# One encoder layer in float32 on one core: the stores to HBM move from the load queue to ScalarE's queue

## The chip, the cores and the metric

The kernel runs on one core of a Trainium2 chip. The metric is device time in microseconds (us) of one execution; the time of the kernel before is the median of three runs. A core has five engines, each with its own in-order instruction stream: TensorE (PE, matmuls), VectorE (DVE), ScalarE (ACT), GpSimd (POOL) and SyncE (SP), which computes nothing and here issues the DMA transfers. An instruction that waits for a semaphore holds up everything behind it in its own stream, and nothing in the others.

## What is computed

One layer, applied to a prompt of 1024 tokens and a sample of 512 tokens with the same weights, everything in float32. The core of the reference:

```
h = rms_norm(x, pre_g);  z = h @ w_in                       # 2048 -> 5632
q, k, v, g_attn, u, vg, g_gmlp = split(z)
q, k = rope(q), rope(k)                                     # 8 heads of 128, 2 kv heads
a = window_attention(q, k, v, sink) * silu(g_attn)          # band of 3 blocks of 128, a sink logit
m = spatial_gating(gelu(u), gelu(vg), ln, ws, bs) * silu(g_gmlp)
y = concat([a, m]) @ w_out                                  # 2048 -> 2048
x = x + rms_norm(y, post_g)
x = x + sigmoid(x @ w_pg) * (p @ w_pe)
```

## The kernel before

All arrays lie transposed, features on the 128 partitions and the 1536 tokens of both sequences along the free dimension, in two halves of 768 tokens. The large products go through five sweeps, "a", "b" and "c" (parts of w_in), "y" (w_out) and "p" (w_pg). Each sweep takes its product as a two by two block product with seven block products (the tables `A_OF` and `B_OF` say which quarters are added or subtracted for each, `ORDER` in which order they run). An item is one output pair in one of the seven products: TensorE runs 8 k-tiles by 2 token groups by 3 matmuls into one PSUM tile `ps...` (two of them exist). The three matmuls (lines 171 to 173) are the float32 product from a high and a low part of each operand: ScalarE copies a tile into a rounded high part (line 163), VectorE subtracts to get the low part (line 165, seen as L155).

Around each item stand, on other engines:

- the weights of the item three ahead (`make_weights`): two loads into `wr...` (4 buffers), GpSimd adds or subtracts them, then the split into `wt...` (3 buffers);
- the operands of the next product (`fetch_operand`, `split_operand`): two loads into `ar...`, VectorE adds, then the split into `a...` (8 buffers) as each k-tile is done with;
- the product's way out of PSUM (`leave_product`): ScalarE copies to `u...` or `v...` (lines 255, 269, 275) and VectorE adds, which gives outputs `o...`; from there, by kind, rope (VectorE and GpSimd), Gelu, Silu, squares, transposes, and then a store to a scratch tensor in HBM (`q`, `k`, `v`, `gu`, `vg`, `y`) or to the output.

Attention and the spatial gating run as small jobs between the items of sweeps "b" and "c". They load what earlier sweeps stored (`aq`, `ak`, `av`, `vn`, `gm`) and store their own results (`at<-ao`, `gum<-mx`). In sweep "p" the tiles `x2` (residual plus normed y) are made and stored as well (`x<-x`). At the start the kernel makes p @ w_pe into scratch tensors (`pe<-pe`), and the normed x (`h<-x`, `h<-xb`).

The order of everything is fixed when the kernel is built: the class `Line` keeps a clock of TensorE's planned time and runs the jobs that are due; each job is a generator that yields the time it expects its step to take. So the place of an instruction in its engine's stream is the planner's estimate of when its inputs are ready.

All DMA goes out from SyncE: `load` at line 139 issues on `nc.sync`, and `store` is the same function (line 142). Both kinds therefore stand in one stream, in the planner's order: 1374 loads and 304 stores. The framework adds the waits: a store waits for the engine that made its data; a load waits until its buffer is free; and each DMA takes one of eight completion counters in turn (`DMAHW0` to `DMAHW7` in the listings below) and waits until the DMA that had that counter before it, eight places back, has landed.

Of the kernel before, what the change touches and what calls it, by code (L numbers as in the profile page):

```python
# [96 lines left out]
def tile_encoder_layer(ctx: ExitStack, tc: tile.TileContext, xT, pT, wall, pre_g, post_g, sink,  # L97
                       ln_g, ln_b, wsT, bs, cos, sin, mask, out):
    nc = tc.nc
# [39 lines left out]
    def load(dst, src):  # L139
        nc.sync.dma_start(out=dst, in_=src)  # L140

    store = load

    ident = const.tile([P, P], F32, tag="ident", name="ident")
    make_identity(nc, ident)
# [821 lines left out]
```

## Time and profile before

| | |
|---|---|
| three runs | 2611.05 us median (2610.92 to 2614.11) |
| the profiled execution | 2611.79 us, of which its span from the first to the last instruction 2610.0 us |
| TensorE busy | 2503.3 us, 96% of the span |
| VectorE, ScalarE, GpSimd busy | 1703.8 us (65%), 958.4 us (37%), 736.8 us (28%) |
| DMA | 643.63 MB through one queue, packets take 72.7% of the 16 engines' span, 247 GB/s from and to HBM |

Busy time counts the engine's own work. Waiting and the issuing of DMAs by a sequencer are not in it, so SyncE has no busy time at all; its waits are a view of their own. Idle time of an engine other than TensorE costs something only where TensorE then waits for it.

### The profile page before, as it was taken

What the parts mean: (1) busy time and instruction counts of PE and PEld (TensorE: products, weight loads), DVE (VectorE), ACT (ScalarE), POOL (GpSimd) and SP (SyncE); (2) the same over time, 40 slices, a digit from 0 to 9 for tenths busy, and PEclk for the clock granted to TensorE, in tenths of its full rate; (3) what the DMA queues carried; (4) which work ended last, traced back from release to release, by engine and by line L of the source; (5) the groups of instructions that cost most, each with busy time, mean ns of one, the idle gap of its engine ahead of it and who ended that gap; (6) DMA issues with size and microseconds to landing.
All of it is one profiled execution on the core that took longest, in us unless ns stands there. A gap on an engine that the chain in (4) does not pass through costs nothing.

```text
span 2610.0 us, 36511 instructions
## 1 busy us (share of the span) xinstructions
PE 2503.3 (96%) x14268; PEld 2462.0 (94%) x14268; DVE 1703.8 (65%) x1883; ACT 958.4 (37%) x1378; POOL 736.8 (28%) x316
## 2 busy tenths in 40 slices
PE   5998999999999999999999999999999999999998
PEld 5998999999989999999999999999999999999998
DVE  3657566766667757777767665465566876666773
ACT  3142222323675543333546732332232223322321
POOL 4164324355012202302222013112310321433434
PEclk8999999999999999999999999999999999999999
DMA  6967776666575679879656677566577987879885
GB/s 228 360 237 239 259 248 218 202 206 235 181 263 183 186 245 298 308 252 308 211 173 223 215 269 256 211 224 222 171 233 253 332 302 287 284 246 318 306 301 204
DMA packets 372109, 645.97 MB, mean 248 GB/s; under 512 B 29280, under 2 KB 211680, under 8 KB 371936
## 3 DMA queue, kind: packets, MB, share of 16 engines
q1 hardware_dynamic: 371936, 643.63, 72.7%
q8 instruction: 112, 1.84, 0.3%
q14 instruction: 61, 0.50, 0.1%
HBM read 533.43 MB, written 110.10 MB: 247 GB/s over the span
## 4 chain that ended last, share of the span: by engine, by line
PE 71%; DVE 12%; ACT 5%; issue 5%; POOL 3%; DMA 3%; SPq 0%; POOLq 0%; DVEq 0%; ACTq 0%
PE psy L172 5%; PE psy L173 5%; PE psy L171 5%; PE psp L172 5%; PE psc L173 5%; PE psc L172 5%; PE psp L173 5%; PE psc L171 5%; PE psp L171 5%; PE psa L172 4%; PE psa L171 4%; PE psa L173 4%; PE psb L172 3%; PE psb L173 3%; PE psb L171 3%
## 5 line engine op out<-in xcount | busy, mean ns | idle before, releaser
L171 PE MATMUL psa<-aa,wta 128*128 128x384 f32 x896 | 304.8, 340 | 9.0 <-DVE oa L152 5.2
L172 PE MATMUL psa<-aa,wta 128*128 128x384 f32 x896 | 304.2, 339 | 3.2 <-DVE aa L155 3.2
L171 PE MATMUL psy<-ay,wty 128*128 128x384 f32 x896 | 303.1, 338 | 4.1 <-ACT ay L163 4.1
L171 PE MATMUL psc<-ac,wtc 128*128 128x384 f32 x896 | 305.9, 341 | 1.0 <-ACT ac L163 1.0
L172 PE MATMUL psp<-ap,wtp 128*128 128x384 f32 x896 | 301.6, 337 | 4.6 <-DVE ap L155 4.6
L172 PE MATMUL psy<-ay,wty 128*128 128x384 f32 x896 | 303.1, 338 | 2.2 <-DVE ay L155 2.2
L171 PE MATMUL psp<-ap,wtp 128*128 128x384 f32 x896 | 301.5, 337 | 3.8 <-ACT ap L163 3.8
L172 PE MATMUL psc<-ac,wtc 128*128 128x384 f32 x896 | 301.5, 337 | 1.7 <-DVE ac L155 1.7
L173 PE MATMUL psa<-aa,wta 128*128 128x384 f32 x896 | 303.0, 338 | 0.0
L173 PE MATMUL psy<-ay,wty 128*128 128x384 f32 x896 | 302.3, 337 | 0.0
L173 PE MATMUL psc<-ac,wtc 128*128 128x384 f32 x896 | 301.4, 336 | 0.0
L173 PE MATMUL psp<-ap,wtp 128*128 128x384 f32 x896 | 300.8, 336 | 0.0
L171 PE MATMUL psb<-ab,wtb 128*128 128x384 f32 x672 | 230.7, 343 | 0.5 <-DVE ua L152 0.5
L172 PE MATMUL psb<-ab,wtb 128*128 128x384 f32 x672 | 226.2, 337 | 2.5 <-DVE ab L155 2.5
L173 PE MATMUL psb<-ab,wtb 128*128 128x384 f32 x672 | 225.9, 336 | 0.0
L171 PEld LDWEIGHTS psa<-aa,wta 128*128 128x128 f32 x896 | 170.9, 191 | 10.7 <-issue 4.8
L172 PEld LDWEIGHTS psa<-aa,wta 128*128 128x128 f32 x896 | 170.9, 191 | 5.6 <-DVE aa L155 5.4
L172 PEld LDWEIGHTS psp<-ap,wtp 128*128 128x128 f32 x896 | 169.3, 189 | 6.7 <-DVE ap L155 6.4
L171 PEld LDWEIGHTS psy<-ay,wty 128*128 128x128 f32 x896 | 170.6, 190 | 4.9 <-ACT ay L163 4.8
L172 PEld LDWEIGHTS psy<-ay,wty 128*128 128x128 f32 x896 | 170.5, 190 | 4.1 <-DVE ay L155 3.8
L171 PEld LDWEIGHTS psp<-ap,wtp 128*128 128x128 f32 x896 | 169.3, 189 | 4.9 <-ACT ap L163 4.7
L172 PEld LDWEIGHTS psc<-ac,wtc 128*128 128x128 f32 x896 | 169.5, 189 | 2.5 <-DVE ac L155 1.9
(254 smaller groups left out, 5432.3 us busy)
## 6 DMA issues: line engine op xcount, KB each, us to landing
wrc<-wall SPq DMA_DIRECT2D x96, 512.0 KB, 7.0
arb<-h SPq DMA_DIRECT2D x96, 384.0 KB, 6.1
arc<-h SPq DMA_DIRECT2D x96, 384.0 KB, 5.5
wry<-wall SPq DMA_DIRECT2D x72, 512.0 KB, 6.0
wrp<-wall SPq DMA_DIRECT2D x72, 512.0 KB, 7.2
arp<-x SPq DMA_DIRECT2D x88, 384.0 KB, 5.8
wra<-wall SPq DMA_DIRECT2D x60, 512.0 KB, 5.7
ara<-h SPq DMA_DIRECT2D x80, 384.0 KB, 5.4
```

What stands on the lines that cost most here:

```text
L171: nc.tensor.matmul(ps, lhsT=l[0], rhs=r[0], start=start, stop=False)
L172: nc.tensor.matmul(ps, lhsT=l[0], rhs=r[1], start=False, stop=False)
L173: nc.tensor.matmul(ps, lhsT=l[1], rhs=r[0], start=False, stop=stop)
```

## The change

The name `store` becomes a function of its own, which issues on ScalarE's queue. Loads stay on SyncE.

```
@@ -139,7 +139,8 @@
     def load(dst, src):
         nc.sync.dma_start(out=dst, in_=src)
 
-    store = load
+    def store(dst, src):
+        nc.scalar.dma_start(out=dst, in_=src)
```

The streams of TensorE, VectorE and GpSimd keep their instructions and their order. SyncE loses 304 DMAs (1678 become 1374), and ScalarE's stream grows from 1284 to 1588 rows. The eight completion counters are still dealt out over all DMAs in program order, loads and stores together. Line numbers after line 142 are one higher in the changed kernel.

On SyncE near the end of the p @ w_pe stage, before the change (names with `h` or `pe` on the left are stores to scratch tensors, `wra_1` are the weights of the second item of sweep "a"):

```order
L140 DMA pe_1_132<-pe_1_869 128x768 [waits DMAHW5_49,DVE_49]
L140 DMA h_4_168<-x_12_354 128x768 [waits DMAHW6_49]
L140 DMA pe_0_133<-pe_0_887 128x768 [waits DMAHW7_49,DVE_49]
L140 DMA wra_1_10_903<-wall 128x4x128 [waits DMAHW0_49,Activation_49]
L140 DMA wra_1_10_903<-wall 128x4x128 [waits DMAHW1_49]
L140 DMA wra_1_11_906<-wall 128x4x128 [waits DMAHW2_49,Activation_49]
L140 DMA wra_1_11_906<-wall 128x4x128 [waits DMAHW3_49]
L140 DMA h_5_169<-x_13_356 128x768 [waits DMAHW4_49]
```

The same place on SyncE after the change:

```order
L140 DMA sin<-sin 128x1024 [waits DMAHW3_49]
L140 DMA wra_1_10_903<-wall 128x4x128 [waits DMAHW5_49,DVE_49]
L140 DMA wra_1_10_903<-wall 128x4x128 [waits DMAHW6_49]
L140 DMA wra_1_11_906<-wall 128x4x128 [waits DMAHW4_49,DMAHW0_49,Pool_49]
L140 DMA wra_1_11_906<-wall 128x4x128 [waits DMAHW2_49]
L140 DMA wra_2_10_1039<-wall 128x1024 [waits DMAHW2_49,DMAHW0_49,Pool_49]
```

The stores between the table `sin` and the weights are gone from this stream; the loads still wait for completion counters, which stores on the other queue hold in between.

On ScalarE in the second product of sweep "a" (number 5 in `ORDER`; `va` are copies out of PSUM, `wta` splits of weights), before:

```order
L269 ACTIVATE va_1952<-psa_3_1871 128x768
L163 ACTIVATE wta_6_1978<-wra_6_11_1892 128x1024
L269 ACTIVATE va_2030<-psa_4_1948 128x768
L163 ACTIVATE wta_7_2060<-wra_7_11_1968 128x1024
L269 ACTIVATE va_2108<-psa_5_2026 128x768
```

The same stretch after (`q` is a rope result from GpSimd, `h` a normed x tile from VectorE):

```order
L270 ACTIVATE va_1952<-psa_3_1871 128x768 [waits PE_49]
L143 DMA q_0_188<-oa_5_1878 128x768 [waits DMAHW4_49,Pool_49]
L143 DMA h_6_186<-xb_1867 128x768 [waits DMAHW7_49,DVE_49]
L164 ACTIVATE wta_6_1978<-wra_6_11_1892 128x1024
L143 DMA h_7_187<-xb_1912 128x768 [waits DMAHW6_49,DVE_49]
L270 ACTIVATE va_2030<-psa_4_1948 128x768 [waits PE_49]
L143 DMA q_0_188<-oa_5_1954 128x768 [waits DMAHW7_49,Pool_49]
L143 DMA h_0_180<-xb_1944 128x768 [waits DMAHW0_49,DVE_49]
L164 ACTIVATE wta_7_2060<-wra_7_11_1968 128x1024 [waits DMAHW2_49]
L143 DMA h_1_181<-xb_1990 128x768 [waits DMAHW5_49,DVE_49]
L270 ACTIVATE va_2108<-psa_5_2026 128x768 [waits DMAHW3_49,PE_49]
```

Two stores now stand ahead of each copy out of PSUM or each split, and each waits for VectorE or GpSimd.

On ScalarE at the end of the fifth product of sweep "a" (number 4 in `ORDER`; `aa` are splits of the next product's operands, `oa_4_3854` a Gelu whose result TensorE transposes), before:

```order
L275 ACTIVATE va_2183<-psa_6_3781 128x768
L163 ACTIVATE aa_0_3868<-ara_0_10_3361 128x768
L529 ACTIVATE oa_4_3854<-oa_4_3854 128x768
L163 ACTIVATE wta_1_3880<-wra_1_00_3804 128x1024
L163 ACTIVATE aa_1_3883<-ara_1_10_3428 128x768
```

The same place after:

```order
L276 ACTIVATE va_2183<-psa_6_3781 128x768 [waits DVE_49]
L143 DMA q_0_190<-oa_4_3785 128x768 [waits DMAHW4_49,Pool_49]
L164 ACTIVATE aa_0_3868<-ara_0_10_3361 128x768 [waits PE_49]
L530 ACTIVATE oa_4_3854<-oa_4_3854 128x768 [waits DMAHW6_49]
L164 ACTIVATE wta_1_3880<-wra_1_00_3804 128x1024 [waits DMAHW7_49,DMAHW6_49,Activation_49]
L164 ACTIVATE aa_1_3883<-ara_1_10_3428 128x768 [waits PE_49]
```

One store of a rope result, which waits for GpSimd, has come in ahead of the burst of operand splits.

## Rows read from the trace of the kernel before

**Rows 1.** The page, busy time of each engine, share of the span, instructions.
```profile
PE 2503.3 (96%) x14268; PEld 2462.0 (94%) x14268; DVE 1703.8 (65%) x1883; ACT 958.4 (37%) x1378; POOL 736.8 (28%) x316
```

**Rows 2.** Waits of TensorE: who waited for whom, us in total, times, longest.
```profile
PE pspe L171 <- ACT pa L163: 11.7, 1, 11.7
PE ss_x L291 <- POOL accx L152: 11.6, 2, 10.4
PE s L172 <- DVE ks L155: 8.6, 8, 2.1
PE t L652 <- ACT p L645: 5.4, 19, 1.6
...
PE psa L171 <- DVE oa L152: 5.2, 2, 4.5
```

**Rows 3.** Waits of SyncE's own queue, same columns.
```profile
SPq L140 <- ACT ao L676: 200.8, 22, 15.9
SPq L140 <- DVE x L152: 115.6, 32, 9.5
...
SPq L140 <- POOL op L152: 78.4, 16, 10.4
```

**Rows 4.** Line 140: DMA instructions, duration ns min/median/max, first and last start us.
```profile
L140 SPq DMA_DIRECT2D pe<-pe x32: 319/504/1896, 18.8 to 115.6; - x32
...
L140 SPq DMA_DIRECT2D gum<-mx x32: 319/320/596, 992.4 to 1225.2; - x32
```

**Rows 5.** Timeline from 95 us: start, length, engine, instruction, [idle before <- releaser].
```profile
95.54 3.39 SPq L140 DMA_DIRECT2D wra<-wall  x4
...
103.94 2.40 POOL L155 TENSOR_TENSOR wra<-wra,wra 128x1024 f32<-128x1024 f32 x1 [29.94 <-DMA wra<-wall]
...
106.38 1.06 ACT L163 ACTIVATE wta<-wra 128x1024 fp32r<-128x1024 f32 x1 [31.27 <-POOL wra L155]
...
107.47 1.23 DVE L155 TENSOR_TENSOR wta<-wra,wta 128x1024 fp32r<-128x1024 f32 x1 [3.31 <-ACT wta L163]
...
108.61 1.81 DVE L385 COPY pe<-pspe 128x768 f32<-128x768 f32 x2
...
109.71 0.41 PE L171 MATMUL psa<-aa,wta 128*128 128x384 f32 x1 [2.38 <-ACT aa L163]
```

**Rows 6.** Windows: stretch, engines' busy us (instructions), clock, DMA share, GB/s.
```profile
80.00:107.00 27.00, 27.00 (x158) 26.87 (x156) 18.12 (x21) 0.62 (x1) 2.40 (x1) 1.00 0.99 372
```

**Rows 7.** Timeline, 238 to 248 us.
```profile
238.68 0.81 ACT L269 ACTIVATE va<-psa 128x768 f32<-128x768 f32 x1 [6.56 <-PE psa L173]
...
243.10 2.59 DVE L428 SCALAR_TENSOR_TENSOR xb<-xb,pre_sb,rb_x 128x768 f32<-128x768 f32 x1
...
245.73 0.96 DVE L155 TENSOR_TENSOR ara<-ara,xb 128x768 f32<-128x768 f32 x1
...
246.61 0.95 DVE L152 TENSOR_TENSOR oa<-ua,psa 128x768 f32<-128x768 f32 x1
```

**Rows 8.** Timeline from 464 us.
```profile
464.31 0.84 ACT L163 ACTIVATE aa<-ara 128x768 fp32r<-128x768 f32 x1
464.49 2.44 POOL L152 TENSOR_TENSOR oa<-oa,rbq 128x768 f32<-128x768 f32 x1
465.04 0.84 ACT L529 ACTIVATE oa<-oa 128x768 f32<-128x768 f32 x1
...
466.42 0.81 PE L492 MATMUL tnvg<-ident,oa 128*128 128x128 f32 x6
...
466.96 0.32 SPq L140 DMA_DIRECT2D q<-oa  x1
```

**Rows 9.** Timeline in attention, 763 to 774 us.
```profile
763.12 0.32 SPq L140 DMA_DIRECT2D gu<-ob  x1
...
767.45 0.63 ACT L577 ACTIVATE qs<-aq 128x512 fp32r<-128x512 f32 x1 [0.87 <-DMA aq<-q]
...
773.25 0.45 PE L172 MATMUL s<-ks,qs 128*128 128x384 f32 x1 [2.09 <-DVE ks L155]
```

## The prediction

> **What bounds the kernel now.** I read the page first. TensorE is busy 2503.3 of 2610.0 us [rows 1], so all that any change of queues can win is its idle time, some 107 us, and whatever is lost must show up there too. The next view is TensorE's waits [rows 2]: the two longest, 11.7 us for the first split of the kernel and 11.6 us for GpSimd's sum of squares, hang on the start of the kernel and on a chain of adds, and no store stands in them. Of the rest, 8.6 us is attention's scores waiting for VectorE's low part of k, 5.4 us transposes waiting for ScalarE's scaled probabilities, 5.2 us a product waiting until VectorE has read PSUM. No row has TensorE waiting for a DMA directly, so a load counts only through the engine that works on it.
>
> Then SyncE's own waits [rows 3]. Here the reader is to see how long the single stream stands before a store: 200.8 us in 22 cases for the attention output, 115.6 us in 32 for the x2 tiles, 78.4 us in 16 for outputs finished on GpSimd, the longest single stand 15.9 us. Everything behind, loads included, waits that long. The change takes these stands out of SyncE's stream and puts them into ScalarE's, which is busy only 37% [rows 1], but on which every operand split, every weight split and half of the copies out of PSUM stand in order.
>
> **What goes and what it is worth.** SyncE's loads may now pass a store that isn't ready. Not freely: each DMA still waits for the one eight places back, and where that is a store, the load waits for its landing. So a load gains up to seven places. Whether that reaches TensorE I looked up where TensorE stood and a late load was behind it.
>
> The end of the first stage is one [rows 5]. SyncE issues the four loads of the second item's weights at 95.54 us, GpSimd, which has stood 29.94 us for them, adds at 103.94, ScalarE splits at 106.38, VectorE takes the low part at 107.47 and only then, behind it in order, the two copies out of PSUM at 108.61, for which TensorE waits 2.38 us. With the loads earlier the split is no longer held by GpSimd; it is then held by the stores that now stand ahead of it on ScalarE. In that stretch the 16 DMA engines are busy 99% of the time at 372 GB/s [rows 6], so a store of 384 KB is moved in about 1 us and the loads can't simply come in between. Bounds: 0, when the same bytes lie ahead, and 2.38, when the wait goes altogether; I take the middle, 1.2.
>
> The Trainium skill, page "DMA: Bandwidth & Descriptors", section "Issuing engines are not separate DMA queues", speaks against this gain: DMAs started on several engines run on the same 16 DMA engines and interleave, and the only thing saved is the time to start them. By that rule this term and the next are 0 and the sum below is 2.2 us higher. The trace has both cases: the 99% stretch agrees with it, and the 15.9 us stand is not one of transfer at all.
>
> The other is in attention [rows 9]. A store of a Gelu result leaves SyncE at 763.12, the loads of q and k right behind it; ScalarE waits 0.87 us for them, and the scores wait 2.09 us on TensorE. Bounds 0 and 2.09, near the row where the DMA is named as the releaser (0.87): taken 1.0. In the other blocks the splits of q and k come long after their loads, so I count nothing more of the 8.6 us.
>
> **What is added to ScalarE.** 304 DMA instructions. On SyncE such a store holds the sequencer 0.32 us in the median when the queue is free and 0.50 us when it is crowded [rows 4]; no DMA was issued from ScalarE before, so this is the nearest row, and 0.33 us is what I take. The total, 304 by 0.32 to 0.50, is 97 to 153 us in a stream with some 1650 us of idle time, and weight splits run up to two items ahead of their use, so nearly all of it is hidden. What isn't hidden are the waits, and only where the next instruction on ScalarE is one that TensorE needs at once. I laid the new order of ScalarE over the times of its old instructions and of the stores' producers. Three places come out.
>
> First, the second product of sweep "a" [rows 7]. VectorE is behind there and runs without a gap. A store of normed x ahead of the copy `va` needs VectorE's x tile, which ends at 245.69 us; the copy, 238.68 before, can then start only at 245.69 + 0.33 + some wake-up = 246.1 and ends at 246.9. VectorE wants its result at 246.61. So of the 7.4 us by which the copy slips VectorE's lateness takes up 7.1, and 0.3 us come out. The same pattern one item earlier gives another 0.3 to 0.4. TensorE waits for just this VectorE instruction (the 5.2 us row of rows 2 has it). Together +0.7; bounds 0 and 5 times 0.5 = 2.5, with each of the five items hit at the dearer issue price.
>
> Second, the burst of splits at the end of the fifth product [rows 8]. The store of a rope result comes in ahead of the split at 464.31. GpSimd finishes that tile at 464.49 + 2.44 = 466.93; with 0.33 for the issue the split starts at about 467.3, 3.0 us late, and so does all behind it. The Gelu at 465.04 then ends at 468.9 in place of 465.9, and TensorE, which began its six transposes at 466.42, would begin them 2.5 us later. VectorE's low parts move along, so nothing catches up before the next product. +2.5; bounds 0 (if the loads that are no longer held let GpSimd finish sooner) and 3.0.
>
> Third, attention. In each of the 24 blocks a store of the output stands among short steps that follow each other closely: the transposes wait 5.4 us in 19 cases already [rows 2], a mean of 0.3 us, so there is no room there. Where the store falls between the Exp of the sink and the scaled probabilities, 0.33 us goes through to TensorE; I find that in about one block in four, 6 by 0.33 = +2.0; bounds 0 and 24 by 0.5 = 12.
>
> In the last sweep weight splits slip by some microseconds, since stores of outputs wait for GpSimd in front of them (78.4 us over 16 cases on SyncE [rows 3]). An item is 48 matmuls, and 2503.3 us by 14268 [rows 1] is 0.175 us each, so 8.4 us; a split that may run from two items ahead has up to 16.8 us of cover, and I count nothing. If that cover were gone, the 78.4 us would come down on TensorE. The last store of the kernel moves to an idle ScalarE: 0.
>
> **The sum.** −1.2 − 1.0 + 0.7 + 2.5 + 2.0 = +3.0 us on the profiled execution's own 2611.79 us (2610.0 of span and 1.8 around it) gives 2614.8. That execution is 0.74 us above the median of the runs shown, so against the median the forecast is 2614.0 us, 0.1% more. About 0.2%, 5.2 us, is what a measurement of this kernel can tell from no change: 2605.8 to 2616.3 counts as the same.
>
> **Rivals.** A, faster: the loads were the hidden cause of more than I grant. Breaking the stands lets GpSimd and VectorE run ahead everywhere, and the waits that hang on them shrink: the 2.38 us, the 5.2 us, the 8.6 us. Together 16.2; with 5.2 of costs still paid, 2611.05 − 16.2 + 5.2 = 2600. For it: stands of 200.8 us in attention alone. Against: in nearly all blocks ScalarE's splits are not waiting for a load.
>
> B, slower: the convoy. Where VectorE has no idle time, ScalarE waits for VectorE at a store, and VectorE then waits for the copy or split behind that store, so that each store of the early rope and x tiles opens a gap in the engine that was the bound there. Some 36 such stores (16 of x, 20 of q and k) at 0.5 us are 18 us: 2629. It decides from the point where VectorE's lateness no longer covers ScalarE's slip; at 246.61 it covers 7.1 of 7.4 us. For it: the margin is that thin. Against: behind 270 us VectorE has idle time again.
>
> C, it doesn't do what it says: since a load still waits for the DMA eight places back, and its buffer often was a store's source, SyncE is held by the same stores as before, only a little later, and ScalarE's waits lie in its idle time: 2611.
>
> **How the numbers follow.** Forecast 0.43, with its own range 2608 to 2619; A 0.20; B 0.25; C 0.12. Faster by over 0.2%: A alone, 0.20. Slower: B and about a quarter of the forecast's range (2616.3 to 2619), 0.25 + 0.11 = 0.36. Same: the rest, 0.44. For 8 in 10 the range has to reach to near the middle of A and past B's price, since 12 us stood as the upper bound of attention alone: 2602 to 2632.
>
> **What would show it.** In the changed kernel's profile a second hardware queue has the 304 stores, and SyncE's list of waits no longer has `ao`, `op` or the x2 tiles. TensorE's wait at 109.7 us is about 1.2 us or less, the one near 773 us under 1.1. Near 466 us the transposes wait some 2.5 us where they began without a wait. GpSimd's waits for weights fall. The waits on `t` go up by about 2 us. I am wrong if TensorE's waits move by more than 6 us in total in either direction; if DMA instructions on ScalarE take 0.6 us or more; or if TensorE waits for weight splits anywhere in the last sweep.

## The result, and the profile after

The changed kernel takes 2627.71 us in the median of six runs (2619.0 to 2630.7); the kernel before took 2610.99 us in six runs beside them. The ratio is 1.0056 (the two medians alone would give 1.0064), with a 95% interval of 1.0038 to 1.0073: the change makes the kernel slower by about half a per cent. The forecast was 2614.0 us, so the direction on which it was built is right and the size is not: 16.7 us came instead of 3.0. The profiled execution took 2629.63 us.

The page after, engines as in [rows 1], then the two hardware queues (packets, MB, share of the 16 engines' span):

```profile
PE 2504.5 (95%) x14268; PEld 2462.5 (94%) x14268; DVE 1694.8 (64%) x1883; ACT 958.8 (36%) x1378; POOL 751.6 (29%) x316
...
q1 hardware_dynamic: 306144, 533.51, 61.3%
q10 hardware_dynamic: 65792, 110.12, 11.2%
```

TensorE works as long as before (2504.5 us for 2503.3). Its idle time is the span less that: 2627.8 − 2504.5 = 123.3 us, where it was 2610.0 − 2503.3 = 106.7. The 16.6 us between them are nearly all of the 17.8 us by which the span grew, so the question is which waits grew. The waits of TensorE after, to be laid beside [rows 2]:

```profile
PE pspe L172 <- DVE pe L386: 16.3, 8, 12.8
...
PE t L653 <- ACT p L646: 10.7, 17, 3.5
...
PE psp L173 <- DVE ap L156: 7.6, 8, 4.0
PE s L173 <- DVE ks L156: 7.0, 7, 2.6
PE psa L173 <- DVE aa L156: 6.4, 9, 2.0
PE psa L172 <- DVE oa L153: 6.0, 2, 4.6
PE tnvg L493 <- ACT oa L530: 4.4, 2, 2.4
```

The first row is new in its size: a single wait of 12.84 us at the start, in the p @ w_pe stage, where it was 3.04 before:

```profile
31.04 0.44 PE L171 MATMUL pspe<-pa,wtpe 128*128 128x384 f32 x1 [3.04 <-DVE pe L385]
```

SyncE's stream did lose the stands of [rows 3]; in their place stand others, some on the landing of the very stores that left:

```profile
SPq L140 <- DVE wta L156: 95.6, 29, 8.4
SPq L140 <- DMA gum<-mx: 81.5, 19, 11.1
SPq L140 <- POOL wra L153: 79.4, 19, 12.1
```

And a store on ScalarE costs what [rows 4] let expect, 0.33 us (line 143, duration ns min/median/max):

```profile
L143 ACTq DMA_DIRECT2D pe<-pe x32: 326/326/389, 30.3 to 120.4; - x32
...
L143 ACTq DMA_DIRECT2D at<-ao x24: 366/377/417, 667.1 to 1521.4; - x24
```

**The start.** The timeline from 14 us after, ScalarE's own rows and those of SyncE, VectorE and TensorE that matter:

```profile
14.74 2.29 ACT L321 ACTIVATE sq<-x 128x768 f32<-128x768 f32 x3
...
17.27 0.96 DVE L386 COPY pe<-pspe 128x768 f32<-128x768 f32 x1 [1.37 <-PE pspe L174]
...
20.98 4.72 SPq L140 DMA_DIRECT2D wra<-wall  x4
...
30.31 0.35 ACTq L143 DMA_DIRECT2D pe<-pe  x1
30.71 0.84 ACT L321 ACTIVATE sq<-x 128x768 f32<-128x768 f32 x1 [13.67 <-DMA wra<-wall]
...
38.06 1.04 ACT L164 ACTIVATE wtpe<-wrpe 128x1024 fp32r<-128x1024 f32 x1
...
41.28 0.69 PE L172 MATMUL pspe<-pa,wtpe 128*128 128x384 f32 x1 [12.84 <-DVE pe L386]
```

VectorE has the first `pe` tile ready at 17.27 + 0.96 = 18.2 us. The store of it leaves ScalarE at 30.31. What ended the wait is named one row further down: a landing of `wra<-wall`, a load of weights that neither the store nor the square behind it reads. It is the store's completion counter. In ScalarE's stream and in SyncE's stand (the first number is the place in the stream):

```
ScalarE
12 L143 DMA pe_0_111<-pe_0_404 128x768 [waits DMAHW2_49,DVE_49]
SyncE
24 L140 DMA wrpe_428<-wall 128x1024 [waits DMAHW7_49]
...
27 L140 DMA wra_0_10_673<-wall 128x4x128 [waits DMAHW2_49]
...
34 L140 DMA lnb<-ln_b 128x8x1 [waits DMAHW1_49]
35 L140 DMA cos<-cos 128x1024 [waits DMAHW2_49]
```

With no store in its stream SyncE has nothing to hold it, and eleven loads (places 24 to 34) get their counters before the first store does. The store's counter, DMAHW2, belongs until its landing to the second half of a weight load, which SyncE issues only at 21.88 us, 3.7 us after the tile was ready, and which by the trace lands at 30.23. (What stands ahead of the prediction, that the counters are dealt in program order, holds within one queue; across the two queues, to judge by this listing, they follow the order in which the framework expects the DMAs to start.) ScalarE stands for that landing, and with it nine squares and the weight split `wtpe`, which came at 27.81 us before and comes at 38.06 now.

**The last sweep.** The same pattern, with new waits of TensorE. VectorE ends the x2 tile at 2392.09 + 0.96 = 2393.05; SyncE issues a load `arp<-x` at 2392.37, which has the store's counter and takes 5.8 us to land, that is until 2398.1; the store leaves at 2398.21:

```profile
2392.09 0.96 DVE L153 TENSOR_TENSOR x<-x,y 128x768 f32<-128x768 f32 x1
...
2392.37 0.43 SPq L140 DMA_DIRECT2D arp<-x  x1
...
2398.21 0.33 ACTq L143 DMA_DIRECT2D x<-x  x1
2398.73 1.06 ACT L164 ACTIVATE wtp<-wrp 128x1024 fp32r<-128x1024 f32 x1 [12.36 <-PE psp L174]
...
2399.82 1.22 DVE L156 TENSOR_TENSOR wtp<-wrp,wtp 128x1024 fp32r<-128x1024 f32 x1 [6.78 <-ACT wtp L164]
...
2409.43 0.44 PE L173 MATMUL psp<-ap,wtp 128*128 128x384 f32 x1 [1.35 <-DVE ap L156]
...
2419.54 0.69 PE L173 MATMUL psp<-ap,wtp 128*128 128x384 f32 x1 [3.99 <-DVE ap L156]
```

The store goes 5 us later than its tile allowed, and the weight split behind it too. VectorE stands 6.78 us for that split and then has its low part, the copies out of PSUM and the low parts of the operands to do in one go; the low parts come late, and TensorE waits 1.35, 0.34 and 3.99 us within 10 us.

These 5.7 us are not the whole price, for after the longest wait TensorE runs at the lower of its two clock levels (1.2 GHz). In the rows of windows (as [rows 6], the granted clock is the third number from the end) it is 0.50, then a mean of 0.59:

```profile
2419.00:2422.00 3.00, 2.46 (x8) 2.46 (x9) 1.45 (x3) 1.06 (x1) 0.00 (x0) 0.50 0.97 298
2422.00:2426.00 4.00, 4.00 (x16) 4.00 (x15) 3.26 (x4) 1.97 (x3) 0.00 (x0) 0.59 1.00 348
```

There the matmuls start 0.32 us apart instead of 0.17. From 2407.06 to 2425.15 us TensorE starts the matmuls that it started from 2396.07 to 2405.08 before: 18.1 us for 9.0, so this place costs 9.1 us. The profile counts slow matmuls as busy time.

Near 381 us, in sweep "a", a row behind a store of normed x (`h<-xb`) names the load in so many words, though it reads another tile:

```profile
381.35 0.33 ACTq L143 DMA_DIRECT2D h<-xb  x1
381.88 1.06 ACT L164 ACTIVATE wta<-wra 128x1024 fp32r<-128x1024 f32 x1 [10.46 <-DMA ara<-h]
```

### The profile page after: what moved, and what is told of

It is laid out like the page before. It is cut to its first block, busy times and chain, and to the rows that moved or that the text cites. A ratio compares the mean times of both kernels' runs of the same rounds, so it can differ in the third digit from the quotient of the medians.

```text
span 2627.8 us, 36495 instructions
## 1 busy us (share of the span) xinstructions
PE 2504.5 (95%) x14268; PEld 2462.5 (94%) x14268; DVE 1694.8 (64%) x1883; ACT 958.8 (36%) x1378; POOL 751.6 (29%) x316
## 4 chain that ended last, share of the span: by engine, by line
PE 63%; DVE 11%; DMA 8%; issue 7%; ACT 5%; POOL 5%; SPq 1%; ACTq 0%; POOLq 0%; DVEq 0%
PE psc L174 5%; PE psc L173 5%; PE psc L172 5%; PE psy L173 5%; PE psy L174 5%; PE psy L172 5%; PE psb L172 3%; PE psb L173 3%; PE psb L174 3%; PE psp L173 3%; PE psp L172 3%; PE psp L174 3%; PE psa L173 3%; PE psa L174 2%; PE psa L172 2%
## 5 line engine op out<-in xcount | busy, mean ns | idle before, releaser
L173 PEld LDWEIGHTS psa<-aa,wta 128*128 128x128 f32 x896 | 170.2, 190 | 9.7 <-DVE aa L156 9.6
L172 PEld LDWEIGHTS psa<-aa,wta 128*128 128x128 f32 x896 | 170.3, 190 | 8.8 <-ACT aa L164 5.4
L174 PEld LDWEIGHTS psa<-aa,wta 128*128 128x128 f32 x896 | 170.3, 190 | 0.0
```

Source lines behind the costliest of these rows:

```text
L172: nc.tensor.matmul(ps, lhsT=l[0], rhs=r[0], start=start, stop=False)
L173: nc.tensor.matmul(ps, lhsT=l[0], rhs=r[1], start=False, stop=False)
L174: nc.tensor.matmul(ps, lhsT=l[1], rhs=r[0], start=False, stop=stop)
```

## The experiments

Theory 1, formed from these rows: the loss is made of stores that hold ScalarE, at the start because SyncE runs ahead. Theory 2: it is the issue time, 304 times 0.33 us. A third, a convoy, is that ScalarE waits for the makers of the tiles. Ratios are to runs of the kernel before on the same chip. "Changed kernel" in the diffs is the kernel with all stores on ScalarE.

**One kind back on SyncE.** Against the changed kernel:

```
-        store(pe_d[j][h], o)
+        load(pe_d[j][h], o)
```

> All stores on ScalarE's queue except the 32 of p @ w_pe (`pe<-pe`), which stay on SyncE. Theory 1 (run-ahead): at the start SyncE, with no store in its stream, issues 18 loads and tables before the first `pe` store is counted, and that store waits on ScalarE for one of them to land; ScalarE's squares and splits stand behind it. With the `pe` stores back on SyncE the wait of TensorE for `pspe` at 41 us (12.84 us) falls back to about 3 us, the one at 110 us may come back (2.4 us), the rest stays: 2627.7 - 9.8 + 0 to 2.4, that is 2618 to 2620. Theory 2 (issue time): 32 of 304 issues of 0.33 us are gone and a tenth of the loss with them: 2626. A gap of 12 us that stays says that another store than `pe` or another cause holds the start.

2617.26 us, ratio 1.0023 (1.0006 to 1.0039). The wait at the start is 3.40 us; the loss is less than half of what it was. But the wait at 110 us, which was gone in the changed kernel, is back, and longer than the 2.38 us of [rows 5]:

```profile
31.57 0.69 PE L172 MATMUL pspe<-pa,wtpe 128*128 128x384 f32 x1 [3.40 <-DVE pe L386]
...
110.49 0.66 PE L172 MATMUL psa<-aa,wta 128*128 128x384 f32 x1 [3.22 <-ACT aa L164]
```

**Only that kind moved.** Against the kernel before:

```
-        store(pe_d[j][h], o)
+        nc.scalar.dma_start(out=pe_d[j][h], in_=o)
```

> Only the 32 `pe<-pe` stores on ScalarE's queue, all others on SyncE. Here SyncE can run ahead by one load of weights only, since the next thing in its stream is a store of normed x. Theory 1 (run-ahead): the first `pe` store waits for nothing but VectorE's copy, TensorE's wait for `pspe` stays at about 3 us, and the time is that of the kernel before within 3 us, 2609 to 2614, maybe with the 2.4 us at 110 us gained. Rival (convoy): ScalarE stands still because it waits for VectorE's copies of `pspe` at each store, whatever SyncE does; then the 10 us at the start are here too: 2619 to 2622.

2613.13 us, ratio 1.0006 (0.9993 to 1.0020): no difference that can be measured. The same 32 stores that cost some 8 us beside the others cost nothing that can be measured when SyncE is held by its own stores. So ScalarE's waits for VectorE's copies aren't the cause; what SyncE does meanwhile is. The wait at the start is 5.17 us, 2.1 more than before, and the longest wait for the sum of squares behind it is 2.5 us shorter (7.9 for 10.4). The waits on `t` in attention add up to 7.6 us in this run, where it was 5.4, though no store of attention was moved: that row varies by some 2 us without a cause there.

```profile
32.92 0.69 PE L171 MATMUL pspe<-pa,wtpe 128*128 128x384 f32 x1 [5.17 <-DVE pe L385]
```

**SyncE paced.** Against the changed kernel:

```
+    pace = scratch("pace", [1, 32 * P])
...
         store(pe_d[j][h], o)
+        load(pace[:, (2 * j + h) * P:(2 * j + h + 1) * P], o[0:1, 0:P])
```

> All stores on ScalarE's queue as in the changed kernel; beside each of the 32 `pe` stores SyncE writes 512 bytes of the same tile to a scratch tensor of its own, so that SyncE's stream is held at the same places as in the kernel before while the large stores and their waits on ScalarE stay as they are. Theory 1 (run-ahead): TensorE's wait for `pspe` near 41 us falls from 12.84 to 3 to 5 us, and the time to 2617 to 2621. Rival (convoy, ScalarE waits for VectorE at each store): the wait stays at 10 us or more, 2626 to 2629.

At the place it was made for theory 1 holds: 5.01 us where 12.84 stood, with every store still on ScalarE. The time doesn't follow: 2625.73 us, ratio 1.0063 (1.0039 to 1.0087), near what the rival had said. With the 32 small writes in SyncE's stream a wait of 6.87 us opens at the end of the stage, where there was none in the changed kernel; that the writes make it was not tested. The run shows what makes the wait at the start, not a way out.

```profile
33.14 0.69 PE L172 MATMUL pspe<-pa,wtpe 128*128 128x384 f32 x1 [5.01 <-DVE pe L388]
...
114.47 0.66 PE L172 MATMUL psa<-aa,wta 128*128 128x384 f32 x1 [6.87 <-DVE pe L388]
```

**The x2 stores back on SyncE.** Against the changed kernel:

```
-        store(x2_d[k][h], x)
+        load(x2_d[k][h], x)
```

> All stores on ScalarE's queue except the 32 of the x2 tiles in the last sweep (`x<-x`), which stay on SyncE. Theory 1 says of the last sweep: a store of x2 stands on ScalarE ahead of four splits of operands and waits there for VectorE's add, so the low parts come late and TensorE waits 1.35, 0.34 and 3.99 us near 2410 to 2420. Without these stores on ScalarE the three waits go: 2627.7 - 5.7 = 2622, less if SyncE, held by x2 stores again, brings the loads later. Theory 2 (issue time): 32 issues less, 2626 or no change that can be measured, and the three waits stay.

2618.91 us, ratio 1.0030 (1.0017 to 1.0043). The three waits between 2409 and 2420 us are gone (the row of `ap` falls from 7.6 to 2.0 us), the start is as bad as in the changed kernel.

```profile
PE pspe L172 <- DVE pe L386: 17.1, 8, 13.6
...
PE psp L173 <- DVE ap L156: 2.0, 5, 0.6
```

**The issue time alone.** Against the kernel before; `junk` is a 128x256 tile in bfloat16:

```
-    store = load
+    def store(dst, src):
+        nc.sync.dma_start(out=dst, in_=src)
+        nc.scalar.activation(junk, junk, AF.Copy)
```

> The kernel before, all stores on SyncE; at each of the 304 places where the changed kernel issues a store on ScalarE, ScalarE does a small copy of its own that waits for nothing (128x256, an estimate of 0.33 us from 0.84 us for 768 and 1.06 us for 1024 columns). It is the issue time of the stores alone. The prediction's term for it is +2.0 us (attention), so 2613; theory 2 (issue time is the loss) wants most of the 16.7 us: 2621 to 2628. Theory 1: +0 to +4, 2611 to 2615, with the extra in the waits on `t`.

2615.26 us, ratio 1.0014 (1.0005 to 1.0024): +3.7 us by the ratio, a quarter of the loss, and that with copies of 0.40 us, which is more than a store takes. It is an upper bound: a store can be issued while the activation ahead of it still runs (in the changed kernel one at 42.13 us, beside a square that runs from 42.07 to 42.92), a copy can't. The waits on `t` go from 5.4 to 6.4 us, less than that row varies by itself.

```profile
L147 ACT ACTIVATE junk<-junk x304: 395/402/420, 17.4 to 2604.0; 128x256 bf16<-128x256 bf16 x152
...
PE t L657 <- ACT p L650: 6.4, 22, 1.5
```

**Issue time and the wait for the maker.** The same, but the copy reads the tile that is stored:

```
+        part = src[:, 0:2, :] if len(src.shape) == 3 else src[:, 0:2 * P].rearrange(...)
+        nc.scalar.activation(junk, part, AF.Copy)
```

> As the run with small copies on ScalarE, but each copy reads 256 columns of the tile that is stored, so that it waits for the tile's maker as the store does. Stores, counters and SyncE's stream stay those of the kernel before. Theory 1: the start is not hurt (there it is run-ahead of loads, which is not here), while the losses behind it are waits for the makers: at 481 us 2.4, attention 3 to 5, the last sweep 5.7: together +8 to +14, 2619 to 2625. Rival (all of it is counters and the order of DMAs): as the copies that wait for nothing, 2611 to 2615.

2618.52 us, ratio 1.0024 (1.0012 to 1.0036), a little under what theory 1 had said, and the places correct it. The wait of the transposes is there, 2.31 us at 473 us. The last sweep is not: the longest wait there for VectorE's low part is 1.6 us, where the changed kernel has 4.0, and the start is that of before.

```profile
473.19 0.33 PE L497 MATMUL tnvg<-ident,oa 128*128 128x128 f32 x1 [2.31 <-ACT oa L534]
...
PE psp L177 <- DVE ap L160: 4.3, 5, 1.6
```

So theory 1 was half wrong. In the last sweep it isn't the x2 tile that this store waits for, as its expectation had it, but the counter, as at the start: ready at 2393.05, issued at 2398.21, on the landing of `arp<-x`. By these two runs the issue is worth at most 0.14%, the makers another 0.10%, and what is left of 0.56%, 0.32% or some 8 us, comes with the stores themselves: counters, landings and SyncE's run-ahead. The intervals overlap, so the shares are rough.

**The stores that hurt back on SyncE.** Against the changed kernel the two edits above, and

```
         yield 3.0
-        store(dst, o)
+        load(dst, o)
         qkv_left[0] += 1
```

> The 32 stores of p @ w_pe, the 32 of x2 and the 20 of rope results (q, k) go back to SyncE; the other 220 stay on ScalarE's queue. Theory 1 (run-ahead at the start, waits for other engines' tiles behind it): the wait near 41 us is 3 us, those near 480 (2.36) and 2409 to 2420 us (5.7) are gone; against the run that had only the `pe` stores back (ratio 1.0023 to the kernel before, 1.0006 to 1.0039) another 6 us go, to 2609 to 2613, no difference to the kernel before that can be measured. Theory 2 (issue time): 220 issues are left of 304, and the time stays above 2615.

2606.83 us, ratio 0.9978 (0.9964 to 0.9993). The wait at 41 us is 3.1 us again, those at 481 and 2409 to 2420 us are gone, those on `s` fall from 8.6 to 4.9 us, those on `t` stay higher than before:

```profile
PE t L653 <- ACT p L646: 8.1, 19, 1.9
...
PE s L173 <- DVE ks L156: 4.9, 6, 1.2
```

**The same kernel on another chip.**

> The same kernel as the run with three kinds of stores back on SyncE, on another chip. TensorE's waits in that run's trace add up to 96.5 us against 98.6 in the kernel before, 2 us less, while its median was 6.4 us lower; TensorE's own busy time was 5.3 us lower in the profiled execution, for which the change gives no reason. If only the waits are the change's doing: a ratio of 0.999 (2611). If the gain is whole: 0.9978 again.

2610.45 us, ratio 0.9991 (0.9975 to 1.0007). The gain did not come again whole. In its trace TensorE is idle for 2608.0 − 2501.9 = 106.1 us, in the first one for 2602.6 − 2498.0 = 104.6, before for 106.7: the waits account for 0.6 to 2 us. Most of the 5.3 us of busy time is the clock: summed over the clock records of the traces, TensorE works 58.1 us at the lower level in the first execution, 66.4 in the repeat and 66.9 before. The kernel is as fast as before; whether it is faster by a tenth of a per cent can't be told from these runs.

**Only ScalarE's own results on ScalarE** (60 of the 304 stores). Against the kernel before, `store_a` issues on `nc.scalar`:

```
-        store(at_d[g][h][:, :, off:off + P]...
+        store_a(at_d[g][h][:, :, off:off + P]...
-        store(dst, t.rearrange("p (t d) -> p t d", t=HB))
+        store_a(dst, t.rearrange("p (t d) -> p t d", t=HB))
-            store(gu_d[i][h], o)
+            store_a(gu_d[i][h], o)
```

> Only stores of tiles that ScalarE itself has just made go on its queue: 24 attention outputs (`at<-ao`), the transposed v and vg tiles, and the Gelu results (`gu`); the other stores stay on SyncE. No such store can wait for another engine's work, and SyncE no longer stands 200.8 us for the attention outputs. Theory 1: no loss, at most the issue time (+0 to 2 us); a gain of up to 2 us if SyncE's stands held loads that TensorE missed (the scores at 773 us): 2608 to 2613. Rival (in attention a store on ScalarE costs whatever it waits for, through its counter or the 0.33 us): the waits on `t` rise from 5.4 to 9 us or more as they did with all stores there, 2614 to 2617.

2612.44 us, ratio 0.9997 (0.9988 to 1.0006). The 200.8 us for which SyncE stood for the attention output are gone, and the time does not fall. The waits on `t` are 8.7 us, near what the rival had said, those on `s` 7.9, and the time is the same all the same.

```profile
PE t L655 <- ACT p L648: 8.7, 21, 2.1
PE s L175 <- DVE ks L158: 7.9, 7, 2.6
```

**The same stores, planned later.** Against the changed kernel, `pe` on SyncE as above, and

```
-        yield 1.8
+        yield 5.8
         store(x2_d[k][h], x)
...
-        yield 3.0
+        yield 7.0
         store(dst, o)
```

> The `pe` stores are on SyncE; all others stay on ScalarE's queue, but the stores of x2 and of the rope results are planned 4 us later, so that they stand behind more of ScalarE's splits and their tiles are done when they come to the head; the order of all other instructions is the same. Theory 1 (the store waits for its maker and holds the splits behind it): the waits of TensorE near 480 (2.36 us) and 2409 to 2420 us (5.7) go or halve, as if these stores were back on SyncE: 2610 to 2614. Theory 2 (issue time or the DMA's own traffic, which are the same here): no change against the run that had only the `pe` stores back, 2617.

2612.02 us, ratio 0.9998 (0.9985 to 1.0011). With 272 stores on ScalarE, and their bytes and issue time as they were, no loss is left against the kernel before. (Against the run with only the `pe` stores back, 1.0023 with 1.0006 to 1.0039, the intervals just overlap; the waits tell the two apart.) The wait of 2.36 us at the transposes is gone, and that of 3.99 us is 0.88:

```profile
2399.32 0.44 PE L173 MATMUL psp<-ap,wtp 128*128 128x384 f32 x1 [0.88 <-DVE ap L156]
```

The holds themselves are still there. The store of x2 that stood 5 us in the changed kernel has its tile at 2377.16 + 0.96 = 2378.12 and leaves at 2381.33, again on the landing of the load `arp<-x` that has its counter. But the weight split is now ahead of it, and the operand splits come only at 2383.74:

```profile
2374.43 1.06 ACT L164 ACTIVATE wtp<-wrp 128x1024 fp32r<-128x1024 f32 x1 [7.25 <-DMA wrp<-wall]
...
2377.16 0.96 DVE L153 TENSOR_TENSOR x<-x,y 128x768 f32<-128x768 f32 x1
...
2381.33 0.33 ACTq L143 DMA_DIRECT2D x<-x  x1
2383.74 0.85 ACT L164 ACTIVATE ap<-arp 128x768 fp32r<-128x768 f32 x1 [8.25 <-PE psp L174]
```

Over the whole trace the stores on ScalarE stand some 57 us for their counters, counted from when the tile is ready and ScalarE has come to the store (worked out from the trace's landings); in the changed kernel it is some 50 us. So the sum of these holds doesn't decide the time; the rows show a cost where a hold stands ahead of a split that another engine needs at once.

**One more kind back.** Against the kernel with three kinds back:

```
-            store(hn[0][k // 8][k % 8], x0[k])
+            load(hn[0][k // 8][k % 8], x0[k])
```

> The stores of p @ w_pe, x2, rope results and, in addition, the 16 of the first normed x (`h<-x`) are on SyncE; 204 stores stay on ScalarE. With h on ScalarE TensorE waited 3.72 us at 111 us and 4.19 us for `rb_x` at 203 us, against 2.38 and 2.65 before. If SyncE's run-ahead past the h stores makes these, both go back and the time is 2 to 3 us below the run it is compared with: 2605 to 2609. If they come from the other stores on ScalarE, no difference to it.

2611.26 us, ratio 1.0000 (0.9985 to 1.0015). The two waits named do go down (2.83 us at 111 us, 2.67 us for `rb_x`), but in the repeat of the kernel with three kinds back `rb_x` was 2.62 us already, and the time is the same. These two aren't shown to hang on the h stores.

## Why the prediction was right and wrong

- **What bounds the kernel.** Right: TensorE's work did not change, and the loss is its idle time, together with the lower clock that follows a long wait and that the sum doesn't price.
- **What was costed at nothing.** Here it failed. The step read: "each DMA still waits for the one eight places back, and where that is a store, the load waits for its landing". It was applied to loads alone. The other direction was left out: a store on ScalarE waits for a load that SyncE has just issued, and then everything behind it on ScalarE does. The two largest losses are of that kind, 12.84 − 3.04 = 9.8 us at the start and 5.7 us of waits (9.1 with the clock) in the last sweep; neither place has a term in the sum. The first went when SyncE was held (3.40, 5.17 and 5.01 us), the second when the x2 stores were back or stood later.
- **Last sweep: "I count nothing".** For the stores of outputs to which it spoke this held: they stayed on ScalarE in the runs without a loss. What it left out are the stores of x2 in the same sweep. It counted the cover of weight splits, while the low parts of four operands came behind such a split on VectorE, and TensorE waited for those.
- **−1.2 at 109.7 us.** In the changed kernel the whole wait of 2.38 us was gone, and with it the lower clock behind it (0.62 from 109.5 to 114 us before, 1.00 from 119 to 124 us after); TensorE came through this place 4.2 us faster. But the start was 10 us late by then, and where the start is mended the wait is back, with 3.22, 3.72 and 3.29 us. By itself this term gains nothing.
- **−1.0 in attention.** The 2.09 us went: the same scores come at 791 us in the changed kernel and don't wait. The transposes ahead of them in the block wait 3.50 us (at 777.05), where it was 2.12 in four pieces from 758.52 on. By the starts of the same matmuls, from 700 us before to these scores, the changed kernel loses another 2.3 us and the run with 60 stores 0.3: no gain. The scores as a whole went from 8.6 to 7.0 us. The Trainium skill's page "DMA: Bandwidth & Descriptors", section "Issuing engines are not separate DMA queues", says that starting DMAs on several engines saves only the time to start them. By that rule these two terms are 0. At these two places the times agree with it: the first wait came back, and 60 stores moved gave 0.9997.
- **+0.7 in sweep "a".** Right: 1.43 us at 256 us where 0.65 stood.
- **A gain that no term has.** At the ends of two products, near 1560 and 1765 us of the kernel before, TensorE waits 2 to 3 us for operand splits, and the lower clock follows. In all eight traces with the stores of `gum`, `ma` and `mm` on ScalarE (the changed kernel among them) most of that wait is gone; in the five with them on SyncE it is there. By the starts of the same matmuls the changed kernel wins 3.9 and 3.7 us at these places. At 1758 us the rows show GpSimd's add of weights beside two of VectorE's splits, which take 4.03 us; in the changed kernel the add falls elsewhere and they take 1.81 (before, then after):

```profile
1758.25 4.03 DVE L155 TENSOR_TENSOR ay<-ary,ay 128x768 fp32r<-128x768 f32 x2
1758.66 2.81 POOL L152 TENSOR_TENSOR wry<-wry,wry 128x1024 f32<-128x1024 f32 x1 [5.75 <-DMA wry<-wall]
...
1764.94 0.44 PE L171 MATMUL psy<-ay,wty 128*128 128x384 f32 x1 [1.47 <-ACT ay L163]
...
1775.16 1.81 DVE L156 TENSOR_TENSOR ay<-ary,ay 128x768 fp32r<-128x768 f32 x2
```

That this collision makes both waits is argued from the rows, not tested. The losses elsewhere are thus larger than the 16.7 us that are left of them. The kernels in which no loss is left have this gain too: by the starts of the same matmuls they are still 5 to 11 us behind the kernel before at its 1545 us.

- **+2.5 at the transposes.** Right: 2.36 us at 480.83, 2.31 when only the wait for the maker was imitated, none with the rope stores back.

```profile
480.83 0.87 PE L493 MATMUL tnvg<-ident,oa 128*128 128x128 f32 x6 [2.36 <-ACT oa L530]
```

- **+2.0 in attention.** Of the right order: the issue time alone gave at most +3.7 us over the whole kernel; how much of it falls on attention the row of `t` can't tell. In the changed kernel `t` rose by 5.3 us, but it rose by 3.3 in the kernel with 60 stores and by 2.2 in that with the `pe` stores alone, and both have the time of before; so this row alone is no cost.
- **The rivals.** B's time (2629) is near the result, its mechanism isn't: the 16 stores of x tiles that it names stayed on ScalarE in runs with no loss (0.9978 to 0.9998), and 0.10% of waits for makers is 3 us, not 18. A's kind of gain came at the two product ends, at waits that A doesn't name. C had the right piece, the eight counters, and drew from it that nothing would happen.
- **The range.** The result lies inside 2602 to 2632, by luck: the upper end was set past B's price and for the upper bound of attention, and the loss came from neither.
- **The signs.** The issue time, the list of SyncE's waits, the transposes and the scores at 773 us came as named. GpSimd's waits for weights fell for `wra` and `wrp` (together from 306.4 to 263.7 us), not for `wrb` (195.6 to 203.8). By its own measure, TensorE's waits moving by more than 6 us, the forecast was wrong: they moved by 16.6.

What stays open: how the 0.32% divides between waits on counters and the later landing of loads. TensorE's busy time differs between executions by up to 8.8 us (2498.0 to 2506.8) with the same 14268 matmuls; most of that is the clock, since it works 58.1 us at the lower level in the first of these executions and 76.8 in the last.

## What to carry to other kernels

Before stores move to a computing engine, look at what the load queue does once nothing holds it: it runs ahead, and if loads and stores share completion counters, the computing engine stands for loads it doesn't use. A store belongs behind the steps that another engine needs at once, not at the place where its data is planned to be ready; with the first 32 stores left on the load queue, 4 us later in the stream left no loss against the kernel before, while stores went on waiting. A wait of the bounding engine is to be priced with the clock that follows it: 5.7 us of waits in the last sweep cost 9.1. And a long stand of the load queue (here 200.8 us) is worth nothing until a wait of the bounding engine is found behind it.

## What the runs showed that was not expected

- The releaser that the profile names for an instruction can belong to the store ahead of it: a square that reads `x` "waited" 13.67 us for a landing of `wra`, a weight split 10.46 us for one of `ara`.
- The coupling works both ways: the load of `cos`, next on the first store's counter, left SyncE only at 33.95 us, after the store of 30.31 us, which took 3.6 us to land.
- Work of 0.40 us at 304 places of an engine that is busy 37% of the time cost 3.7 us by the ratio, 3% of the 122 us put in.
